# Attention scores of a float32 decoder trunk: 128-partition products with stacked keys in place of 64-partition tiles

## The chip, the cores and the metric

The kernel runs on one core of a Trainium2 chip. The metric is the device time of one execution in microseconds; of several runs the median is taken. A core has five engines that work side by side: TensorE (PE, matrix products; its weight loads are a row of their own, PEld), VectorE (DVE), ScalarE (ACT), GpSimd (POOL) and SyncE (SP, here it only issues DMAs).

## The reference

A trunk of two layers on one sequence of 1024 tokens with 1024 features, in float32. Layer 0 mixes by differential attention, layer 1 by causal pooling over windows of 2, 4, 8 and 16; both add an attention over 256 memory tokens, a gate and an output projection. What the change touches is the score of the differential attention: 12 heads, each with two maps of 64 features, rotated by position, and one value of 128 features.

```python
q = q.reshape(B, S, DA_HEADS, 2, DA_QK_DIM)      # 12 heads, 2 maps, 64
k = k.reshape(B, S, DA_HEADS, 2, DA_QK_DIM)
q = apply_rotary(q, cos, sin)
k = apply_rotary(k, cos, sin)
...
s = jnp.einsum('bqhmd,bkhmd->bhmqk', q_blk, k).astype(jnp.float32) * scale
s = jnp.where(mask, s, -jnp.inf)
p = jax.nn.softmax(s, axis=-1)
w = p[:, :, 0] - lam_full * p[:, :, 1]
return jnp.einsum('bhqk,bkhe->bqhe', w.astype(v.dtype), v)
```

## The kernel before, in words

Activations lie with features on partitions and tokens on the free axis, in two halves of 512 tokens. A float32 operand x of a product is split in two float32r parts, hi = round(x) and lo = x - hi, and a product takes three passes, hi*hi, hi*lo and lo*hi (`mm3`, lines 118 to 123).

The order of TensorE's work is written out by hand (`manual_schedule`, line 77); the instructions of the other engines are ordered by the scheduler. TensorE's base is a stream of projections, planned in `plan` (line 972): for each head the queries, the keys, a gate and the values of the next head, 16 steps of three 512-wide products each. `step(n)` issues the next n steps of it. Between the steps stands the work of the head in hand. `attention_layer` (line 1062) walks each head in 10 positions, one for each pair of query blocks and pair of key blocks: it transposes a block of weights (`turn_weights`, line 885), applies the block turned before (`apply_weights`, line 912), and at the positions listed in `ahead` (line 1065) issues the scores of one query block, some of them for the next head already.

A projected query or key leaves PSUM through `query_evac` (line 768) or `key_evac` (line 787). Both begin with `rotary` (line 755): four ACT copies of 32 partitions swap the halves of the features, DVE multiplies by the cosines, POOL multiplies the swapped copy by the sines, DVE adds. Then the operands of the scores are made, for each map on its 64 partitions:

- the stationary query tile `qa`: hi on the map's own 64 partitions, lo on the other 64 (two ACT and two DVE instructions a half; the factor -1/8 is taken in here);
- the moving key tile `kb`: hi on both halves of the partitions, and a second tile `kl` with the lo of both maps (four ACT copies and two DVE subtractions a half).

`scores` (line 831) takes for each half of the keys two PSUM banks out of three, one for each map. First come two products over 128 partitions ([hi; lo] of the query with [hi; hi] of the key, line 848), then two over 64 partitions (hi of the query with lo of the key, line 853): map 0 on partitions 0 to 63, map 1 on 64 to 127. The width is the number of keys in reach, 256 to 512. DVE adds the mask and takes the row minimum (line 857), two steps of the stream follow, and after both halves ACT takes the exponential with its sum (line 866). `combine` (line 872) makes the difference of the two maps on POOL (line 878) and DVE (line 881).

`prologue` (line 343) fills the start: hidden state, rotary tables (`rope_tables`, whose positions are loaded by a DMA that POOL issues, line 552) and the queries and keys of head 0. Line 297 fills the mask on POOL before that. `reuse_waits="tile"` (line 1067) lets the tiles of later stages take the space of attention tiles as each comes free.

Of the kernel before, what the change touches and what calls it, by code (L numbers as in the profile page):

```python
# [10 lines left out]
F32 = mybir.dt.float32  # L11
# [9 lines left out]
P = 128  # L21
# [27 lines left out]
class Trunk:  # L49
    """Activations are held as [feature on partitions, token on the free axis].  # L50

    A float32 operand x of a matrix product is held as two float32r parts,
    hi = round(x) and lo = x - hi; a product takes the passes hi*hi, hi*lo
    and lo*hi."""
# [49 lines left out]
    def load_split(self, wf, name, cols=D, dve=0, parts=1):  # L104
        """Weights of up to D columns as hi and lo, in parts; VectorE makes the first dve
        columns of lo of each part."""
        nc = self.nc
        wh = self.wpool.tile([P, D], F32R, tag="wh", name=f"wh_{name}")
        wl = self.wpool.tile([P, D], F32R, tag="wl", name=f"wl_{name}")
        n = cols // parts  # L110
        for lo in range(0, cols, n):
            nc.scalar.copy(wh[:, lo : lo + n], wf[:, lo : lo + n])  # L112
            for eng, c in ((nc.vector, slice(lo, lo + dve)), (nc.gpsimd, slice(lo + dve, lo + n))):
                if c.stop > c.start:
                    eng.tensor_tensor(wl[:, c], wf[:, c], wh[:, c].bitcast(F32), op=ALU.subtract)  # L115
        return wh, wl

    def mm3(self, out, sh, sl, mh, ml, first, last):
        """out (+)= s^T m over one contraction tile; s stationary, m moving."""
        nc = self.nc  # L120
        nc.tensor.matmul(out, sh, mh, start=first, stop=False)  # L121
        nc.tensor.matmul(out, sh, ml, start=False, stop=False)  # L122
        nc.tensor.matmul(out, sl, mh, start=False, stop=last)  # L123

# [1 line left out]
    def step(self, n):  # L126
        """Issues the next n steps (of three products with 512 columns) of the stream."""
        self.owed += n
        while self.owed >= 1:
            self.owed -= 1  # L130
            self.count += 1
            if next(self.stream, None) is None:
                self.owed = 0
                return
# [12 lines left out]
    def between(self, fn):  # L147
        """Adds work that is no projection to the stream."""

        def run(w):  # L150
            fn()
            return iter(())

        self.jobs.append((lambda: None, run))
# [17 lines left out]
    def projection(self, src, name, evac, halves=(1, 0)):  # L172
        """Adds the projection onto one tile of columns to the stream."""

        def run(w):
            for half in halves:
                yield from self.project(w, half, name, evac, self.sb if name == "v0" else None)

        self.jobs.append((lambda: self.load_w(src, name), run))

    def projection_pair(self, specs, first, second):
        """Two projections, half 1 of both before half 0, with the calls of first
        and second after the half 1 of each."""
# [33 lines left out]
    def rsqrt_small(self, pool, ms, n, tag, rest=None):  # L217
        """(ms + rest + EPS)^-0.5 of [P, n] tiles of PSUM."""
        x = pool.tile([P, n], F32, tag=f"rsx{tag}", name=f"rsx{tag}")
        self.nc.vector.tensor_scalar(x, ms if rest is None else rest, EPS, None, op0=ALU.add)  # L220
        if rest is not None:
            self.nc.vector.tensor_tensor(x, x, ms, op=ALU.add)
        return self.newton(pool, x, n, tag)

    def newton(self, pool, x, n, tag):
        """x^-0.5 of a [P, n] tile."""
# [13 lines left out]
    def mean_square(self, sqs, ones, n, name, bank=None):  # L240
        """[P token, n] means over the partitions of the sum of sqs, each [P, n*P]."""
# [10 lines left out]
    def diagonals(self, pool, r, n, tag, eng=None):  # L252
        """hi and lo of diag(r[:, j]) for j < n, r being [P, n]."""
# [16 lines left out]
    def spread(self, ds, n, name):  # L270
        """[P, n*P] in PSUM: the diagonals along the free axis, on all partitions."""
# [7 lines left out]
    def broadcast(self, pool, r, n, tag, eng=None):  # L279
        """[P, n*P] in PSUM with r [P token, n] along the free axis, on all partitions."""  # L280
        return self.spread(self.diagonals(pool, r, n, tag, eng), n, f"bc{tag}")

# [60 lines left out]
    def prologue(self, pool):  # L343
        """The first hidden state and the first two projections."""
# [65 lines left out]
    def memory_jobs(self, l):  # L410
        """Adds the keys and values of the memory for layer l to the stream: keys, values."""
# [77 lines left out]
    def mem_means(self):  # L489
        """1 / rms of the memory tokens: by token (rsm), and on all partitions (rsmb)."""  # L490
# [9 lines left out]
    def new_hidden(self, half, d, x, g):  # L500
        """Splits x * g of one [P, HALF] tile into the operands of the next projections."""
# [9 lines left out]
    def accumulate_square(self, pool, x, sums, d, name, tags, alone=False, by=None, add=None):  # L511
        """Adds the squares of tile d of a half to sums; those of the last tile can stay alone."""
# [13 lines left out]
    def row_means(self, pool, sums, half, rest=None):  # L526
        """1 / rms of the tokens of one half, by token; rest: what is to be added to the means."""
# [4 lines left out]
    def row_spread(self, half):  # L532
        """1 / rms of the tokens of one half, on all partitions, in PSUM."""
# [12 lines left out]
    def rope_tables(self, sp):  # L546
        """cos and sin of [32 frequencies on partitions, token], repeated 4 times; worked
        out with a quarter of the tokens on each 32 partitions."""
# [47 lines left out]
    def gate_evac(self, get, box, name):  # L596
        """2 * silu of one projected tile, by halves."""
# [56 lines left out]
    def mem_scores(self, pool, nm, q, kv):  # L654
        """softmax of the scores of 4 query blocks, as [P query, 4, MEM], times 0.5."""
# [47 lines left out]
    def mem_units(self, pool, layer, gates, starts):  # L703
        """The memory attention of all heads, between steps of the stream: the
        unit (head, half) number i goes on when the stream has come to starts[i]."""
# [41 lines left out]
    def play(self, events, until=None):  # L747
        """Issues the events that are due before the stream has come to the step until."""
# [6 lines left out]
    def rotary(self, pool, half, out, name):  # L755
# [4 lines left out]
        for b in range(4):  # L760
            o, i = b * 32, (b ^ 1) * 32
            nc.scalar.copy(rot[o : o + 32, :], out[i : i + 32, :])
        nc.vector.tensor_tensor(f, out, self.cosr[:, cols], op=ALU.mult)
# [4 lines left out]
    def query_evac(self, h, box):  # L768
        """Stationary operands of the scores: [hi; lo] of map 0, [lo; hi] of map 1."""
        nc = self.nc  # L770

        def evac(half, out):
            pool = self.apool
            f = self.rotary(pool, half, out, f"q{h}")
            t = pool.tile([P, 2, HALF], F32R, tag="ka", bufs=3, name=f"qa{h}{half}")
            lo, hi = slice(0, 64), slice(64, 128)
            for m, own, other in ((0, lo, hi), (1, hi, lo)):
                nc.scalar.activation(t[own, m, :], f[own, :], AF.Copy, scale=-QSCALE)
                nc.vector.scalar_tensor_tensor(
                    t[other, m, :], f[own, :], -QSCALE, t[own, m, :].bitcast(F32),  # L780
                    op0=ALU.mult, op1=ALU.subtract,
                )
            box[half] = t
# [3 lines left out]
    def key_evac(self, h, box):  # L787
        """Moving operands: [hi; hi] of each map, and lo of both maps."""
        nc = self.nc

        def evac(half, out):
# [3 lines left out]
            u = pool.tile([P, HALF], F32R, tag="kl", bufs=3, name=f"kl{h}{half}")  # L795
            lo, hi = slice(0, 64), slice(64, 128)
            for m, own, other in ((0, lo, hi), (1, hi, lo)):
                nc.scalar.copy(t[own, m, :], f[own, :])
                nc.scalar.copy(t[other, m, :], f[own, :])  # L799
                nc.vector.tensor_tensor(  # L800
                    u[own, :], f[own, :], t[own, m, :].bitcast(F32), op=ALU.subtract
                )
            box[half] = (t, u)
# [27 lines left out]
    def scores(self, pool, h, i, q, k, st):  # L831
        """exp(score - max) of query block i for both maps, and their row sums."""
# [9 lines left out]
        for kh in range(2 if n > HALF else 1):  # L842
            lo, hi = kh * HALF, min(n, (kh + 1) * HALF)
            kb, kl = k[kh]
            w = slice(0, max(hi - lo, 256))
            sc = [self.sb(f"s{h}{i}{m}{kh}") for m in range(2)]
            for m in range(2):
                nc.tensor.matmul(  # L848
                    sc[m][:, w], q[half][:, m, qs], kb[:, m, w], start=True, stop=False
                )  # L850
            for m in range(2):
                own = slice(64 * m, 64 * m + 64)
                nc.tensor.matmul(  # L853
                    sc[m][:, w], q[half][own, m, qs], kl[own, w], start=False, stop=True
                )
# [16 lines left out]
    def combine(self, i, es, st):  # L872
        """softmax(map 0) - lambda * softmax(map 1) of query block i, in place of map 0."""
# [11 lines left out]
    def turn_weights(self, pool, h, p, jj, w):  # L885
        """[P key, 2 key blocks, 256 query] of the weights of a pair of query blocks."""
# [43 lines left out]
    def attend_post(self, pool, h, half, o, g):  # L930
# [12 lines left out]
        def norm():  # L943
            """The squares summed over the partitions stand on all of them: a quarter of
            the tokens is worked on in each quarter of the partitions."""
# [19 lines left out]
    def run_hooks(self):  # L965
        """Issues what else waits for TensorE, at most one of a kind, when it is due."""
# [5 lines left out]
    def plan(self):  # L972
        """The order of all projections."""
# [88 lines left out]
    def attention_layer(self):  # L1062
        tc = self.tc
        # query blocks whose scores are issued in each of the 10 steps of a head
        ahead = {0: [(0, 2)], 1: [(0, 5)], 2: [(0, 3)], 4: [(0, 0)], 5: [(1, 6)], 6: [(0, 1)], 7: [(1, 7)], 9: [(1, 4)]}
        order = [(p, jj) for p in (3, 2, 1, 0) for jj in range(p + 1)]
        with tc.tile_pool(name="attn", bufs=1, reuse_waits="tile") as pool:
            self.apool = pool
            self.prologue(pool)
# [159 lines left out]
    def out_jobs(self, layer):  # L1229
# [17 lines left out]
        def operand(half, r, t):  # L1247
            """hi and lo of one tile of z; those of layer 1 stay on chip."""
# [175 lines left out]
```

## Time and profile before

| | us |
|---|---|
| three runs | 1879.61, 1881.83, 1885.98 |
| median | 1881.83 |
| span of the profiled execution, first to last instruction | 1881.1 |
| PE busy in it | 1815.2 |
| DVE busy | 1198.1 |
| ACT busy | 899.2 |
| POOL busy | 724.5 |

For the profiled execution the span is the only time that is recorded. It lies between the lowest and the median of the runs. Attention with its start takes the first 885 us or so, the memory's keys and values, the output projection of layer 0, the pooling layer and the last projection the rest.

How to read the rows: a row of a timeline has the start, the duration, engine, source line and operation, what is written and read, the shape, and the idle time of the engine before it with what ended it. Products are pipelined and their ends are modelled, so a 512-wide product shows 0.39 us though the next one starts sooner; the distance from start to start tells what one occupies. A weight load belongs to each product and normally runs during the product before.

### The profile page before, as it was taken

Reading aid. Unit: us, or ns where it says so; the run is one execution under the profiler, and the core shown is the slowest. Engines: PE = TensorE matmul, PEld = TensorE weight load, DVE = VectorE, ACT = ScalarE, POOL = GpSimd, SP = SyncE. Lnnn points to the kernel's source line nnn. Section 1 sums busy time; section 2 is a strip of 40 time slices with the busy share of each in tenths; the row PEclk is TensorE's granted clock in tenths of the full one; section 3 lists DMA queues with packets and bytes.
Section 4 is the critical chain, followed back from the end, with each engine's and each line's share of the span. In section 5 each row is a group of like instructions: output and inputs, shape, how many; then the busy total and the mean of one; then the engine's idle time right before and its main releaser. Section 6 shows DMA issues by size and latency. Waiting matters only on the chain. (4 is left out here: it accounts for less than half of the span.)

```text
span 1881.1 us, 24840 instructions
## 1 busy us (share of the span) xinstructions
PE 1815.2 (96%) x8670; PEld 1457.0 (77%) x8670; DVE 1198.1 (64%) x2446; ACT 899.2 (48%) x1649; POOL 724.5 (39%) x610
## 2 busy tenths in 40 slices
PE   7899999999999999999999999999999999999997
PEld 5577778777777777778788777778887777877885
DVE  7678778778778778876656768645453435454413
ACT  6566566666566657654246655524321112124422
POOL 3244334434444444433253343333332435512452
PEclk9899999999999999999999999999999999999998
DMA  5001111111101111112464769642212121245542
GB/s 181 23 34 39 52 45 51 42 44 57 46 34 57 46 44 47 46 46 68 157 207 140 240 223 301 221 138 93 90 37 94 46 72 58 68 149 201 179 145 95
DMA packets 80956, 186.04 MB, mean 99 GB/s; under 512 B 9120, under 2 KB 17024, under 8 KB 80832
## 3 DMA queue, kind: packets, MB, share of 16 engines
q1 hardware_dynamic: 79440, 182.04, 29.3%
q10 hardware_dynamic: 1296, 2.17, 0.3%
q8 instruction: 68, 1.11, 0.2%
q0 software_dynamic: 96, 0.26, 0.1%
q14 instruction: 56, 0.46, 0.1%
HBM read 152.67 MB, written 31.77 MB: 98 GB/s over the span
## 5 line engine op out<-in xcount | busy, mean ns | idle before, releaser
L866 ACT ACTIVATE e<-e,st 128x640 f32<-128x640 f32 (+4 forms) x192 | 148.2, 773 | 95.9 <-DVE st L857 95.0
L115 POOL TENSOR_TENSOR wl_o<-wf_o,wh_o 128x384 fp32r<-128x384 f32 x64 | 97.3, 1520 | 215.3 <-ACT wh_o L112 199.9
L878 POOL TENSOR_SCALAR e<-e,st 128x640 f32<-128x640 f32 (+4 forms) x96 | 80.7, 841 | 200.1 <-DVE st L877 87.2
L1264 DVE TENSOR_TENSOR zr<-zf,zr 128x512 fp32r<-128x512 f32 x132 | 113.8, 881 | 29.6 <-ACT zr L1263 29.2
L115 DVE TENSOR_TENSOR wl_o<-wf_o,wh_o 128x640 fp32r<-128x640 f32 x64 | 60.2, 940 | 109.3 <-ACT wh_o L112 102.6
L112 ACT CAST wh_o<-wf_o 128x1024 fp32r<-128x1024 f32 x64 | 67.3, 1052 | 113.4 <-PE ob L122 65.2
L857 DVE CUSTOM_DVE_ANT_0 e<-s,mask 128x512 f32<-128x512 f32 (+2 forms) x192 | 107.8, 585 | 16.7 <-PE s L853 15.4
L1263 ACT CAST zr<-zf 128x512 fp32r<-128x512 f32 x132 | 80.7, 620 | 71.8 <-DMA zf<-z 35.7
L906 ACT CAST wth<-wt 128x512 fp32r<-128x512 f32 (+2 forms) x168 | 72.1, 429 | 87.1 <-PE wt L903 71.9
L121 PE MATMUL ga<-hh,wh_ga 128*128 128x512 f32 x256 | 107.9, 422 | 4.2 <-DVE mqf L625 4.2
L121 PE MATMUL pga<-hh,wh_pga 128*128 128x512 f32 x256 | 100.5, 393 | 6.8 <-DVE pz L1188 4.9
L123 PE MATMUL ga<-hh,wl_ga 128*128 128x512 f32 x256 | 101.2, 395 | 0.0
L122 PE MATMUL ga<-hl,wh_ga 128*128 128x512 f32 x256 | 100.9, 394 | 0.0
L122 PE MATMUL ob<-zr,wh_o 128*128 128x512 f32 x256 | 100.3, 392 | 0.0
L121 PE MATMUL ob<-zr,wh_o 128*128 128x512 f32 x256 | 100.3, 392 | 0.0
L123 PE MATMUL ob<-zr,wl_o 128*128 128x512 f32 x256 | 100.3, 392 | 0.0
L122 PE MATMUL pga<-hl,wh_pga 128*128 128x512 f32 x256 | 99.8, 390 | 0.0
L123 PE MATMUL pga<-hh,wl_pga 128*128 128x512 f32 x256 | 99.7, 390 | 0.0
L907 DVE TENSOR_TENSOR wtl<-wt,wth 128x512 fp32r<-128x512 f32 (+2 forms) x168 | 83.1, 495 | 15.1 <-ACT wth L906 14.3
L121 PE MATMUL k<-hh,wh_k 128*128 128x512 f32 x192 | 83.9, 437 | 8.5 <-ACT wh_k L112 7.9
L881 DVE SCALAR_TENSOR_TENSOR e<-e,st,e 128x640 f32<-128x640 f32 (+4 forms) x96 | 82.1, 855 | 9.8 <-POOL e L878 9.0
L848 PE MATMUL s<-kb,qa 128*128 128x512 f32 (+2 forms) x288 | 81.4, 357 | 5.1 <-ACT kb L799 2.7
(283 smaller groups left out, 5480.1 us busy)
## 6 DMA issues: line engine op xcount, KB each, us to landing
zf<-z SPq DMA_DIRECT2D x132, 256.0 KB, 3.9
wf_o<-in_w_out SPq DMA_DIRECT2D x64, 512.0 KB, 3.6
wf_ga<-in_w_in SPq DMA_DIRECT2D x16, 512.0 KB
wf_pga<-in_w_in SPq DMA_DIRECT2D x16, 512.0 KB, 4.3
wf_q<-in_w_in SPq DMA_DIRECT2D x12, 512.0 KB, 3.2
wf_v<-in_w_in SPq DMA_DIRECT2D x12, 512.0 KB, 4.0
z<-rs SPq DMA_DIRECT2D x24, 256.0 KB, 3.2
z<-z SPq DMA_DIRECT2D x24, 256.0 KB, 2.0
```

The lines of the kernel that those rows point to most:

```text
L115: eng.tensor_tensor(wl[:, c], wf[:, c], wh[:, c].bitcast(F32), op=ALU.subtract)
L121: nc.tensor.matmul(out, sh, mh, start=first, stop=False)
L122: nc.tensor.matmul(out, sh, ml, start=False, stop=False)
L123: nc.tensor.matmul(out, sl, mh, start=False, stop=last)
L848: nc.tensor.matmul(sc[m][:, w], q[half][:, m, qs], kb[:, m, w], start=True, stop=False)
L857: nc.vector.tensor_tensor_reduce(out=es[m][:, lo:hi], in0=sc[m][:, : hi - lo], in1=self.mask[:, S - n + lo : S - n + hi], scale=1.0, scala ...
L866: nc.scalar.activation(es[m][:, :n], es[m][:, :n], AF.Exp, bias=least[m], scale=-1.0, accum_out=st[:, 2, m : m + 1],)
L878: nc.gpsimd.tensor_scalar(es[1][:, :n], es[1][:, :n], st[:, 3, 1:2], 1.0, op0=ALU.mult, op1=ALU.mult)
L881: nc.vector.scalar_tensor_tensor(es[0][:, :n], es[0][:, :n], st[:, 3, 0:1], es[1][:, :n], op0=ALU.mult, op1=ALU.add)
L907: nc.vector.tensor_tensor(wl[:, lo:hi], t[:, lo:hi], wh[:, lo:hi].bitcast(F32), op=ALU.subtract)
L1263: nc.scalar.copy(z[:, 0, :], zf)
L1264: nc.vector.tensor_tensor(z[:, 1, :], zf, z[:, 0, :].bitcast(F32), op=ALU.subtract)
```

## The change

The scores keep four products a group, and all run over 128 partitions. The key tile holds [hi; lo] of each map, so that `kl` goes. The query tile `qa` holds [hi; hi], and a second tile holds [lo; zeros], so that the two passes give hi*hi + hi*lo and lo*hi. The tiles with the zeros are four fixed ones, filled on POOL before the prologue; each half of a head writes only the 64 partitions of lo. The two passes of a map now follow each other, map 0 before map 1. The factor -1/8 moves into `rotary`, whose product with the cosines becomes an instruction with a scalar and two tensors for keys and queries alike. The scratch space of POOL's own DMAs is set to 4096, which frees space for the new tiles. The docstrings and comments are dropped without effect on the program.

```diff
-    def rotary(self, pool, half, out, name):
+    def rotary(self, pool, half, out, name, scale=1.0):
...
-            nc.scalar.copy(rot[o : o + 32, :], out[i : i + 32, :])
-        nc.vector.tensor_tensor(f, out, self.cosr[:, cols], op=ALU.mult)
+            nc.scalar.activation(rot[o : o + 32, :], out[i : i + 32, :], AF.Copy, scale=scale)
+        nc.vector.scalar_tensor_tensor(
+            f, out, scale, self.cosr[:, cols], op0=ALU.mult, op1=ALU.mult
+        )
...
     def query_evac(self, h, box):
...
-            f = self.rotary(pool, half, out, f"q{h}")
+            f = self.rotary(pool, half, out, f"q{h}", -QSCALE)
             t = pool.tile([P, 2, HALF], F32R, tag="ka", bufs=3, name=f"qa{h}{half}")
+            z = self.qlo[(2 * h + 1 - half) % len(self.qlo)]
             lo, hi = slice(0, 64), slice(64, 128)
             for m, own, other in ((0, lo, hi), (1, hi, lo)):
-                nc.scalar.activation(t[own, m, :], f[own, :], AF.Copy, scale=-QSCALE)
-                nc.vector.scalar_tensor_tensor(
-                    t[other, m, :], f[own, :], -QSCALE, t[own, m, :].bitcast(F32),
-                    op0=ALU.mult, op1=ALU.subtract,
-                )
-            box[half] = t
+                nc.scalar.copy(t[own, m, :], f[own, :])
+                nc.scalar.copy(t[other, m, :], f[own, :])
+                nc.vector.tensor_tensor(
+                    z[own, m, :], f[own, :], t[own, m, :].bitcast(F32), op=ALU.subtract
+                )
+            box[half] = (t, z)
...
     def key_evac(self, h, box):
...
-            u = pool.tile([P, HALF], F32R, tag="kl", bufs=3, name=f"kl{h}{half}")
             lo, hi = slice(0, 64), slice(64, 128)
             for m, own, other in ((0, lo, hi), (1, hi, lo)):
                 nc.scalar.copy(t[own, m, :], f[own, :])
-                nc.scalar.copy(t[other, m, :], f[own, :])
                 nc.vector.tensor_tensor(
-                    u[own, :], f[own, :], t[own, m, :].bitcast(F32), op=ALU.subtract
+                    t[other, m, :], f[own, :], t[own, m, :].bitcast(F32), op=ALU.subtract
                 )
-            box[half] = (t, u)
+            box[half] = t
...
     def scores(self, pool, h, i, q, k, st):
...
-            for m in range(2):
-                nc.tensor.matmul(
-                    sc[m][:, w], q[half][:, m, qs], kb[:, m, w], start=True, stop=False
-                )
-            for m in range(2):
-                own = slice(64 * m, 64 * m + 64)
-                nc.tensor.matmul(
-                    sc[m][:, w], q[half][own, m, qs], kl[own, w], start=False, stop=True
-                )
+            for m in range(2):
+                for part in range(2):
+                    nc.tensor.matmul(
+                        sc[m][:, w], q[half][part][:, m, qs], k[kh][:, m, w],
+                        start=(part == 0), stop=(part == 1),
+                    )
...
     def attention_layer(self):
...
+            self.qlo = [pool.tile([P, 2, HALF], F32R, name=f"qlo{i}") for i in range(4)]
+            for z in self.qlo:
+                nc.gpsimd.memset(z[64:128, 0, :].bitcast(F32), 0.0)
+                nc.gpsimd.memset(z[0:64, 1, :].bitcast(F32), 0.0)
             self.prologue(pool)
...
-    nc = bacc.Bacc("TRN2", target_bir_lowering=False, num_devices=1)
+    nc = bacc.Bacc(
+        "TRN2", target_bir_lowering=False, num_devices=1, dynamic_dma_scratch_size=4096
+    )
```

More of the change, by code (lines that the diff above doesn't have):

```diff
@@ L843, in scores @@
             lo, hi = kh * HALF, min(n, (kh + 1) * HALF)
-            kb, kl = k[kh]
             w = slice(0, max(hi - lo, 256))
@@ L1062, in attention_layer @@
     def attention_layer(self):
-        tc = self.tc
+        tc, nc = self.tc, self.nc
         ahead = {0: [(0, 2)], 1: [(0, 5)], 2: [(0, 3)], 4: [(0, 0)], 5: [(1, 6)], 6: [(0, 1)], 7: [(1, 7)], 9: [(1, 4)]}
```

## The prediction

> **What bounds the kernel now.** I read the page first (busy shares), then the busy times by stretch, then the groups by form for the two lines of score products, then the TensorE timeline around single score blocks, and last the timelines of the other engines around the operands of the scores.
>
> ```profile
> span 1881.1 us, 24840 instructions
> PE 1815.2 (96%) x8670; PEld 1457.0 (77%) x8670; DVE 1198.1 (64%) x2446; ACT 899.2 (48%) x1649; POOL 724.5 (39%) x610
> ...
> 135.00:885.00 750.00, 747.63 (x3796) 588.11 (x3795) 589.21 (x1518) 465.72 (x915) 309.69 (x305) 1.00 0.14 48
> 885.00:1100.00 215.00, 206.76 (x1065) 173.02 (x1064) 137.47 (x228) 98.89 (x191) 79.51 (x72) 0.99 0.54 178
> ```
>
> The first two lines are the page's; the others give length, then PE, weight load, DVE, ACT, POOL busy, granted clock, DMA share and GB/s. In the steady attention stretch PE is covered for 747.63 of 750 us at full clock; DVE, the next, for 589.21 (79%). So the length of PE's own list sets the end of this stage, and one microsecond taken out of that list should leave the span, as long as what feeds PE keeps up. But "busy" has modelled ends. What a product occupies is better read from start to start.
>
> The changed products are all in this stage. By form (line 848 is the first pass of the scores over 128 partitions, line 853 the second pass over 64):
>
> ```profile
> L853 PE MATMUL s<-kl,qa 64*128 64x512 f32 x144 | 36.2, 500 | 0.0
> L853 PE MATMUL s<-kl,qa 64*128 64x256 f32 x96 | 18.5, 382 | 0.0
> L853 PE MATMUL s<-kl,qa 64*128 64x384 f32 x48 | 10.6, 440 | 0.0
> ```
>
> Two of these belong to one group of four score products, so there are 72 groups 512 wide, 48 of 256 and 24 of 384. Now one group of each width in PE's timeline (start, duration; "x2" is two instructions merged), then a pair of 256-wide products of line 926, and last the weight loads of the first group:
>
> ```profile
> 511.90 0.39 PE L123 MATMUL k<-hh,wl_k 128*128 128x512 f32 x1
> 512.13 0.63 PE L848 MATMUL s<-kb,qa 128*128 128x512 f32 x2
> 512.69 0.51 PE L853 MATMUL s<-kl,qa 64*128 64x512 f32 x2
> 513.12 0.50 PE L121 MATMUL k<-hh,wh_k 128*128 128x512 f32 x1
> 513.46 0.39 PE L122 MATMUL k<-hl,wh_k 128*128 128x512 f32 x1
> ...
> 500.12 0.40 PE L848 MATMUL s<-kb,qa 128*128 128x256 f32 x2
> 500.45 0.39 PE L853 MATMUL s<-kl,qa 64*128 64x256 f32 x2
> 500.77 0.50 PE L121 MATMUL q<-hh,wh_q 128*128 128x512 f32 x1
> 501.10 0.40 PE L122 MATMUL q<-hl,wh_q 128*128 128x512 f32 x1
> ...
> 506.62 0.52 PE L848 MATMUL s<-kb,qa 128*128 128x384 f32 x2
> 507.07 0.44 PE L853 MATMUL s<-kl,qa 64*128 64x384 f32 x2
> 507.44 0.50 PE L121 MATMUL q<-hh,wh_q 128*128 128x512 f32 x1
> 507.79 0.39 PE L122 MATMUL q<-hl,wh_q 128*128 128x512 f32 x1
> ...
> 504.08 0.40 PE L926 MATMUL o<-wth,vh 128*128 128x256 f32 x2
> 504.32 0.40 PE L926 MATMUL o<-wth,vl 128*128 128x256 f32 x2
> ```
>
> ```profile
> 512.69 0.19 PEld L853 LDWEIGHTS s<-kl,qa 64*128 64x128 f32 x2 [0.37 <-issue]
> 513.12 0.19 PEld L121 LDWEIGHTS k<-hh,wh_k 128*128 128x128 f32 x1 [0.25 <-issue]
> ```
>
> A full 512-wide product takes a slot of 0.23 us (511.90 to 512.13), a full 256-wide one 0.12 (two in 504.08 to 504.32). Around line 853 this rhythm breaks at both edges: the second pass starts 0.56 after the first instead of 0.46, its weight load begins only with it, after 0.37 us in which the weight path did nothing, and the product after it again has its load unprepared (0.25 idle) and needs 0.34 instead of 0.23. In between, the two 64-partition products of the pair run at once: both weight loads lie within 0.19 us and the pair leaves PE after 0.43. So line 853 has a gain (two products in one slot) and a cost (two edges).
>
> **The change, part by part.** *TensorE.* Four products stay four, all over 128 partitions and each with its own weights. I price a group as regular slots, from its first product to the second product after it: at 512, 513.46 - 512.13 = 1.33 us against 5 x 0.23 = 1.15, gain 0.18, times 72 is 13.0. At 256, 501.10 - 500.12 = 0.98 against 4 x 0.12 + 0.23 = 0.71, gain 0.27, times 48 is 13.0. At 384, 507.79 - 506.62 = 1.17 against 4 x 0.175 + 0.23 = 0.93 (0.175 is an estimate halfway between the two slots), gain 0.24, times 24 is 5.8. Sum **31.8 us**. That regular slots return is taken from the row of line 848 itself, which follows a projection 0.23 us after it, and from line 926, whose 256-wide products change weights every time and hold 0.12.
> The trace shows that a switch between tile shapes idles the weight path. The Trainium skill, "TensorEngine Tiling (Array Packing)", Key Properties, says that changing the tiling mode drains TensorE while tiles of one mode load and multiply in parallel; by it both edges go, the trace agrees with 0.37 and 0.25 us of idle weight path, and the sum stays at 31.8.
>
> *Operands of the keys.* Before, four ACT copies and two DVE subtractions a half; after, two copies and two subtractions, and the first product needs both halves of the tile, so PE now waits for DVE where it waited for ACT; behind it stands all of PE's list, since that order is written by hand. The tightest place, the second half of the next head's keys before its block 6:
>
> ```profile
> 536.23 0.62 ACT L798 CAST kb<-fk 64x512 fp32r<-64x512 f32 x1 [0.98 <-DVE fk L765]
> 536.88 0.62 ACT L799 CAST kb<-fk 64x512 fp32r<-64x512 f32 x1
> 536.88 0.68 DVE L800 TENSOR_TENSOR kl<-fk,kb 64x512 fp32r<-64x512 f32 x1
> ...
> 538.16 0.62 ACT L799 CAST kb<-fk 64x512 fp32r<-64x512 f32 x1
> 538.17 0.69 DVE L800 TENSOR_TENSOR kl<-fk,kb 64x512 fp32r<-64x512 f32 x1 [0.53 <-ACT kb L798]
> 538.60 0.74 PE L848 MATMUL s<-kb,qa 128*128 128x512 f32 x2
> ...
> 522.42 1.32 DVE L881 SCALAR_TENSOR_TENSOR e<-e,st,e 128x768 f32<-128x768 f32 x1
> ...
> 525.57 0.60 PE L903 MATMUL wt<-cst,e 128*128 128x128 f32 x4
> ```
>
> Now the last copy ends at 538.78, just as PE begins. After: copies 536.23 to 536.85 and 536.88 to 537.50, subtractions 536.88 to 537.56 and 537.56 to about 538.25, if DVE takes them at once. The second map's product comes third in the new order, two slots after the first, so it has about 0.8 us to spare, less some 0.3 that PE arrives earlier (one 256-wide group lies between). I take no new wait. The last two rows give another margin: the weights of block 5 are ready at 523.74 and turned at 525.57, 1.83 us; the groups between shorten that by about half a microsecond.
>
> Lower bound for these waits:
>
> ```profile
>   DVE st L857: 8.5, 20
>   ACT kb L799: 8.5, 12
> ```
>
> These are the waits in front of line 848, loads and products counted together. The first map's bank is complete two products earlier, so DVE can free it earlier, and the key copies shrink; both can go in part. I take 0, with -8 as the lower end.
>
> *Operands of the queries.* ACT gets eight instructions a half instead of six (two copies more, like those of 0.62 us), the keys two fewer, so ACT's sum is unchanged. DVE keeps four, with the scale now in the product with the cosines:
>
> ```profile
> L763 DVE TENSOR_TENSOR fq<-q,trig_tab 128x512 f32<-128x512 f32 x24 | 16.6, 691 | 14.1 <-ACT rotq L762 13.7
> L939 DVE SCALAR_TENSOR_TENSOR og<-o,subln,gaa 128x512 f32<-128x512 f32 x24 | 17.9, 746 | 7.5 <-ACT sq L938 7.4
> ```
>
> The form it takes, read from PSUM, costs 746 ns against 691: 48 x 0.055 = 2.6 us more on DVE, hidden under PE; if that cover were gone it costs just these 2.6.
>
> *Zeros and space.* Eight fills of 64x512 on POOL at the very start:
>
> ```profile
> 0.74 0.95 POOL L297 MEMSET mask<- 128x1024 bf16 x1 [0.29 <-POOLq L1411]
> 1.64 0.73 POOL L552 DMA_DIRECT2D pos_i<-in_positions  x1
> ...
> 7.43 1.27 POOL L524 TENSOR_TENSOR ssqx<-ssqx,ssqx 128x512 f32<-128x512 f32 x1 [4.12 <-ACT ssqx L520]
> ...
> 7.91 0.80 PE L121 MATMUL k<-hh,wh_k 128*128 128x512 f32 x1 [7.91 <-ACT wh_k L112]
> ```
>
> Fills of about 0.5 (half the columns of line 297) to 0.95 us make 4 to 7.6. POOL is idle for 4.12 us before 7.43. Behind them queue the issue of the positions (line 552), on which the rotary tables and through DVE's queue the first hidden state wait, and the first squares. Fully exposed: 7.6; fully covered: 0. I take 1.5, nearer to the idle stretch. The smaller scratch space for POOL's own DMAs touches two issues of this kind, both at the start, and I give it nothing (0.73 if one is issued again). The new tiles take 10 KB a partition more than those they replace and move later tiles; the stretch after attention has 8 us of idle PE (215 - 206.76), and a third of it either way is in the range.
>
> Sum against this execution's span: 1881.1 - 31.8 + 1.5 = 1850.8; the median of the three runs is 0.7 above that span, so 1851.
>
> **The rivals.**
> *A, slower: the parallel pair is lost and the edges stay.* If the idle at the edges belongs to how the score operands are read or signalled and not to the tile's shape, every group gains a slot: 72 x 0.23 + 48 x 0.12 + 24 x 0.175 = 26.5 us, 1908. For it: the pair visibly runs at once. Against it: line 848 reads the same query tile and starts in rhythm, and the product after line 853, which belongs to a projection, is late too. At 512 the edges cost 1.33 - 4 x 0.23 = 0.41 and the parallel slot is worth 0.23, so it decides once more than half of the edge cost stays. The Trainium skill, "TensorE: Matmul & The Clock Gate", Part 3, holds that row tiles run concurrently and a small contraction alone costs as much as a full one; by this rule alone the change goes the way of A. Chance 0.06.
> *B, waits behind DVE take the gain.* The subtraction of the keys, or the row minimum, falls behind a 1.32 us item such as that of line 881, at 12 heads and two places of each: 24 x (1.32 - 0.8) = 12.5 us; behind two such items at one place 12 x (2.64 - 0.8) = 22. Time 1863 to 1873. For it: DVE's list is in fixed order, and at 79% of a shorter stage it would be at 82%. Against it: the margins above. Chance 0.12.
> *C, no change: half of the edge cost stays.* Edge costs worked out as in A are 0.41 at 512, 0.98 - (3 x 0.12 + 0.23) = 0.39 at 256 and 1.17 - (3 x 0.175 + 0.23) = 0.415 at 384. With half of each gone and the parallel slot lost, the gain is 72 x (0.205 - 0.23) + 48 x (0.195 - 0.12) + 24 x (0.21 - 0.175) = 2.6 us; less 1.5 at the start, about 1881 on the median. For and against it stands what stands at A. Chance 0.03. That 64-partition tiles remain can be excluded: the new slices take all partitions.
>
> **How the numbers follow.** My forecast has 0.79. Its own range is 1842 (waits gone) to 1858 (start exposed). The range takes in the first part of B: 1842 to 1866. This kernel's measurement can tell about 0.3%, 5.6 us, from no change; forecast and B are faster by more, so 0.91, C 0.03 within, A 0.06 slower.
>
> **What would show it.** Right: no product with 64 partitions; a 512-wide group and the next product in 1.15 us from start to start, a 256-wide one in 0.71; the next product's load prepared during the group; the attention stage some 32 us shorter with DVE near 82%; all later stages as long as now. Wrong: groups of 1.5 us or more (A); regular groups but PE idle in front of line 848's successor or of the turns, ended by DVE (B); a first product on PE well after 7.91, or longer later stages, which would put the start or the moved tiles in doubt.

## The result and the profile after

The changed kernel takes 1852.24 us in the median (1851.81 to 1856.59, four runs) against 1883.15 for the kernel before (1879.61 to 1885.98, four runs). The ratio is 0.9842, with a 95% interval from 0.9824 to 0.9860: 1.6% faster. In a later comparison on another chip the same kernel (e13) took 1859.40 us, and its ratio was 0.9854 (0.9833 to 0.9876); so between the experiments below, which ran on several chips, the ratios compare better than the microseconds. The profiled execution has a span of 1850.1 us.

The page and the busy times of the attention stretch, now 135 to 860 us (line 851 issues all score products now):

```profile
span 1850.1 us, 24825 instructions
PE 1778.2 (96%) x8670; PEld 1479.3 (80%) x8670; DVE 1223.2 (66%) x2446; ACT 899.7 (49%) x1649; POOL 724.1 (39%) x618
...
135.00:860.00 725.00, 716.18 (x3781) 606.81 (x3781) 609.94 (x1508) 463.69 (x912) 305.28 (x304) 1.00 0.14 50
```

PE has as many instructions as before and is busy 37 us less. DVE stands at 84% of this stretch (79% before), and over the whole span it is busy 25 us more, with as many instructions; where these come from stands in the last section. PE is covered for 716.18 of 725 us, where 747.63 of 750 were covered before: there is idle time now that was not there.

TensorE's timeline around one group of 512 and one of 256, and the weight load of the projection after the first:

```profile
492.93 0.39 PE L851 MATMUL s<-kb,qa 128*128 128x512 f32 x1
493.16 0.39 PE L851 MATMUL s<-kb,qlo 128*128 128x512 f32 x1
493.39 0.39 PE L851 MATMUL s<-kb,qa 128*128 128x512 f32 x1
493.62 0.39 PE L851 MATMUL s<-kb,qlo 128*128 128x512 f32 x1
493.85 0.39 PE L121 MATMUL k<-hh,wh_k 128*128 128x512 f32 x1
494.08 0.39 PE L122 MATMUL k<-hl,wh_k 128*128 128x512 f32 x1
...
495.24 0.28 PE L851 MATMUL s<-kb,qa 128*128 128x256 f32 x1
495.36 0.28 PE L851 MATMUL s<-kb,qlo 128*128 128x256 f32 x1
495.48 0.28 PE L851 MATMUL s<-kb,qa 128*128 128x256 f32 x1
495.60 0.29 PE L851 MATMUL s<-kb,qlo 128*128 128x256 f32 x1
495.72 0.40 PE L121 MATMUL k<-hh,wh_k 128*128 128x512 f32 x1
495.97 0.39 PE L122 MATMUL k<-hl,wh_k 128*128 128x512 f32 x1
```

```profile
493.62 0.19 PEld L121 LDWEIGHTS k<-hh,wh_k 128*128 128x128 f32 x1
```

From the first score product to the second product after the group it is 494.08 - 492.93 = 1.15 us at 512 (1.33 before) and 495.97 - 495.24 = 0.73 at 256 (0.98 before). At 384 it is 488.57 - 487.64 = 0.93 (1.17 before). The load of the projection's weights runs at 493.62, during the last score product, and no longer stands open behind it.

What TensorE lost in the score groups did not all come off the span. The time splits at the first and the last score product; these rows of the two lines of before, and the first and last of line 851 of after, have the starts in the middle ("first to last start"):

```profile
L848 PE MATMUL s<-kb,qa x288: 277/395/770, 65.2 to 879.6; 128*128 128x512 f32 x72, 128*128 128x256 f32 x48, 128*128 128x384 f32 x24
L853 PE MATMUL s<-kl,qa x288: 379/476/792, 67.2 to 879.8; 64*128 64x512 f32 x72, 64*128 64x256 f32 x48, 64*128 64x384 f32 x24
```

```profile
L851 PE MATMUL s<-kb,qa x288: 278/392/522, 60.9 to 849.5; 128*128 128x512 f32 x72, 128*128 128x256 f32 x48, 128*128 128x384 f32 x24
L851 PE MATMUL s<-kb,qlo x288: 277/393/522, 61.3 to 849.7; 128*128 128x512 f32 x72, 128*128 128x256 f32 x48, 128*128 128x384 f32 x24
...
  DVE kb L803: 2.6, 3
```

| | before | after | difference |
|---|---|---|---|
| start to the first score product | 65.2 | 60.9 | -4.3 |
| first to last score product | 814.6 | 788.8 | -25.8 |
| last score product to the end | 1001.3 | 1000.4 | -0.9 |

The last row of the fence is what is left of the waits in front of the score products: 2.6 us, where there were twice 8.5 (loads and products together). From start to start of TensorE's products, what exceeds the regular distance inside the groups adds up to 0.8 us, against 5.3 before. In place of these waits there is a new one, at one place in ten of the twelve heads. Waits of PE in 135 to 850 us, and that place in one head, the turn of the weights of blocks 4 and 5:

```profile
PE wt L902 <- DVE e L880: 8.4, 10, 1.0
```

```profile
503.50 0.91 POOL L877 TENSOR_SCALAR e<-e,st 128x768 f32<-128x768 f32 x1 [3.32 <-DVE st L876]
503.86 0.69 DVE L235 TENSOR_TENSOR rsua<-rsx,rsya 128x128 f32<-128x128 f32 x1
504.37 1.34 POOL L767 TENSOR_TENSOR rotk<-rotk,trig_tab 128x512 f32<-128x512 f32 x1
504.47 0.68 DVE L764 SCALAR_TENSOR_TENSOR fk<-k,trig_tab 128x512 f32<-128x512 f32 x1
505.07 0.79 DVE L236 SCALAR_TENSOR_TENSOR rsua<-rsua,rsya 128x128 f32<-128x128 f32 x1
...
505.78 1.01 DVE L880 SCALAR_TENSOR_TENSOR e<-e,st,e 128x768 f32<-128x768 f32 x1
505.80 0.27 PE L902 MATMUL wt<-cst,e 128*128 128x128 f32 x1
...
506.85 0.55 PE L902 MATMUL wt<-cst,e 128*128 128x128 f32 x3 [0.78 <-DVE e L880]
```

PE turns block 4 at 505.80 and stands until 506.85 for block 5, whose weights DVE finishes at 506.79. POOL was done with its part at 504.41; DVE took the rotation of the keys and two pieces of the norm (lines 235 and 236) first. These two pieces took 0.69 and 0.79 us, while POOL scaled the weights and multiplied the keys by the sines; the same two lines took 0.29 each at 501.63 and 501.95, with POOL idle. Their 0.90 us more are nearly as much as the lack. Counted as before, from the end of DVE's part to the first transpose, the margin of 1.83 us became a lack of 1.0. From start to start, the distances between the transposes of the turns add up to 47.4 us, 11.6 more than before (35.8).

### The profile page after: what moved, and what is told of

Its sections match the earlier page's. It is cut to its first block, busy times and chain, and to the rows that moved or that the text cites. A ratio compares the mean times of both kernels' runs of the same rounds, so it can differ in the third digit from the quotient of the medians.

```text
span 1850.1 us, 24825 instructions
## 1 busy us (share of the span) xinstructions
PE 1778.2 (96%) x8670; PEld 1479.3 (80%) x8670; DVE 1223.2 (66%) x2446; ACT 899.7 (49%) x1649; POOL 724.1 (39%) x618
## 5 line engine op out<-in xcount | busy, mean ns | idle before, releaser
L877 POOL TENSOR_SCALAR e<-e,st 128x640 f32<-128x640 f32 (+4 forms) x96 | 76.3, 795 | 198.0 <-DVE st L876 115.5
L121 PE MATMUL ga<-hh,wh_ga 128*128 128x512 f32 x256 | 104.0, 406 | 3.5 <-DVE mqf L625 3.5
L851 PE MATMUL s<-kb,qa 128*128 128x512 f32 (+2 forms) x288 | 98.5, 349 | 0.9 <-DVE kb L803 0.9
L851 PE MATMUL s<-kb,qlo 128*128 128x512 f32 (+2 forms) x288 | 98.4, 349 | 0.0
L121 PE MATMUL k<-hh,wh_k 128*128 128x512 f32 x192 | 79.2, 412 | 8.5 <-ACT wh_k L112 8.5
```

The source lines that it names most:

```text
L851: nc.tensor.matmul(sc[m][:, w], q[half][part][:, m, qs], k[kh][:, m, w], start=(part == 0), stop=(part == 1),)
L877: nc.gpsimd.tensor_scalar(es[1][:, :n], es[1][:, :n], st[:, 3, 1:2], 1.0, op0=ALU.mult, op1=ALU.mult)
```

## Experiments

**The shape alone, there and back.** The changed kernel with its second pass on the 64 partitions that are not zero, both maps side by side (e1) and map by map (e2).

```diff
-            for m in range(2):
-                for part in range(2):
+            for part in range(2):                  # e2: the two loops as in the changed kernel
+                for m in range(2):
+                    own = slice(64 * m, 64 * m + 64) if part else slice(0, P)
                     nc.tensor.matmul(
-                        sc[m][:, w], q[half][part][:, m, qs], k[kh][:, m, w],
+                        sc[m][:, w], q[half][part][own, m, qs], k[kh][own, m, w],
```

> The changed kernel with its second pass cut back to the 64 partitions that are not zero, both maps side by side as in the kernel before. Theory (the edges belong to the tile shape): groups return to 1.33, 1.17 and 0.98 us with the product after them, 31.8 us more PE time than 1852; where PE is later, the new wait of the turns (11.9 us) may shrink, so 1872 to 1884. Rival (the edges came from how the old operands were read or signalled): the pair in one slot and no edges, 26.5 us less than 1852, about 1826.

> The same 64-partition second pass, but map by map (128, 64, 128, 64 partitions): no pair, four changes of shape in a group instead of two. Theory: each group is regular slots plus twice the edge cost (0.82 us at 512, 0.78 at 256, 0.83 at 384), 72 x 0.82 + 48 x 0.78 + 24 x 0.83 = 116 us more than 1852, less the waits that a later PE no longer meets: 1955 to 1968. Rival (edges not from the shape): about 1852.

e1: 1873.44 us, ratio to the kernel before 0.9945 (0.9920 to 0.9971). e2: 1955.64, ratio 1.0364 (1.0340 to 1.0389). e1 lies where the theory put it. e2 lies at the lower edge of its range; by its ratio, which gives some 1952 us, a few microseconds below it. A 512-wide group of each in TensorE's timeline:

```profile
511.93 0.63 PE L852 MATMUL s<-kb,qa 128*128 128x512 f32 x2
512.49 0.50 PE L852 MATMUL s<-kb,qlo 64*128 64x512 f32 x2
512.92 0.50 PE L121 MATMUL k<-hh,wh_k 128*128 128x512 f32 x1
513.25 0.40 PE L122 MATMUL k<-hl,wh_k 128*128 128x512 f32 x1
```

```profile
518.68 0.40 PE L852 MATMUL s<-kb,qa 128*128 128x512 f32 x1
519.00 0.50 PE L852 MATMUL s<-kb,qlo 64*128 64x512 f32 x1
519.43 0.50 PE L852 MATMUL s<-kb,qa 128*128 128x512 f32 x1
519.86 0.50 PE L852 MATMUL s<-kb,qlo 64*128 64x512 f32 x1
520.29 0.50 PE L121 MATMUL v<-hh,wh_v 128*128 128x512 f32 x1
520.63 0.39 PE L122 MATMUL v<-hl,wh_v 128*128 128x512 f32 x1
```

With the same operands as in the changed kernel, the group of e1 takes 513.25 - 511.93 = 1.32 us, that of the kernel before. In e2, with four changes of shape and no pair, it takes 1.95 (1.97 expected), and each product between two changes takes 0.43 instead of 0.23. e1 differs from the changed kernel in the order of the products too; e2 differs in the shape of the second pass alone. So the edges belong to the change of shape, not to operands or signals, and rival A is out: that row tiles run at once, on which it rested, holds (the two products of e1's pair start within 0.01 us of each other), but does not pay here. The drain on a change of mode that the Trainium skill names ("TensorEngine Tiling (Array Packing)", Key Properties) agrees with this; its size here is 0.4 us for a change there and back, more than the one slot of 0.23 that the pair saves.

e1 has no wait at the turn. There the margin is still positive:

```profile
514.66 2.06 DVE L881 SCALAR_TENSOR_TENSOR e<-e,st,e 128x768 f32<-128x768 f32 x1
...
517.20 0.60 PE L903 MATMUL wt<-cst,e 128*128 128x128 f32 x4
```

517.20 - 516.72 = 0.48 us. Of the 1.35 us between 1.83 and 0.48, DVE's sum itself takes 0.74: 2.06 us here against 1.32 before, both times beside POOL's product with the sines, and 1.01 in the changed kernel, where POOL is idle. The rest comes with the new operands and the order that the scheduler makes of them. From 0.48 to -1.0 it comes with the change of shape, but not by PE's pace alone: in the changed kernel DVE rotates the keys ahead of this sum (504.47), in e1 behind it (516.64). How much each of these takes is not separated.

**Putting the block ahead.** The combination of block 5 at high priority (e3), or its scores one position earlier and those of block 2 one later (e4).

```diff
-                self.combine(i, es, st)
+                with tc.high_priority(offset=SOON):      # e3, for i == 5
+                    self.combine(i, es, st)
...
-        ahead = {0: [(0, 2)], 1: [(0, 5)],
+        ahead = {0: [(0, 5)], 1: [(0, 2)],              # e4
```

> The changed kernel with the combination of block 5 (reciprocal, factor, POOL scaling, DVE sum) put ahead by priority. Theory (the 1.05 us wait of each head's turn of blocks 4 and 5 comes from their place in DVE's order behind the rotation and the norms): that wait goes, 11 x 1.05 = 11.6 us less, about 1841. Rival (the engines have no room there; what is moved back makes PE wait elsewhere): 1848 to 1856.

> The changed kernel with the scores of block 5 issued one position earlier in each head, those of block 2 one later. Theory: the margin before the turn of blocks 4 and 5 grows by about 6.7 us, the wait goes, about 1841. Rival (the five large weight buffers are the limit, block 5 then waits for one to come free): no gain or slower, 1850 to 1865.

e3: 1857.62, ratio 0.9849 (0.9831 to 0.9867), the wait as it was (9.7 us in this trace, 8.4 and 9.7 in the two of the changed kernel); the theory is out. e4: 1868.09, ratio 0.9897 (0.9872 to 0.9923): the wait at the turn is gone, as the theory has it, and a larger one stands before the second map's products, for a PSUM bank that DVE has not yet read, not for a weight buffer as the rival had it:

```profile
PE s L851 <- DVE st L856: 14.4, 20, 1.1
```

So the place of block 5 sets where PE waits; that nothing else was short is refuted.

**Taking work from the engines.** The second query copy on POOL (e6), the lo of the queries on POOL (e11), the norm's small instructions later (e9).

```diff
-                nc.scalar.copy(t[other, m, :], f[own, :])            # in query_evac
+                nc.gpsimd.tensor_copy(t[other, m, :], f[own, :])     # e6
...
-                nc.vector.tensor_tensor(
+                nc.gpsimd.tensor_tensor(                             # e11
                     z[own, m, :], f[own, :], t[own, m, :].bitcast(F32), op=ALU.subtract
...
-DUE = 7
+DUE = 14                                                             # e9
```

> The changed kernel with the second query copy of each map (hi onto the other 64 partitions) made by POOL instead of ACT. Theory (two more ACT copies, 1.24 us, stand in front of block 5's exponentials and take that much of the margin before the turn of blocks 4 and 5): the exponentials start 1.2 us earlier, the 1.05 us wait of each head goes, about 1841. Rival (DVE's order, not ACT's, sets that wait): the wait stays near 1 us, 1850 to 1856.

> The changed kernel with the lo of the queries subtracted on POOL instead of DVE, 48 instructions and some 43 us less on DVE. Theory (the wait of the turn is DVE's lack of room): the wait goes, about 1841. Rival (POOL, which scales the weights of block 5, is then late in its place): the wait stays or grows, 1852 to 1868.

> The changed kernel with the norm of an output half due 14 steps after it instead of 7, which takes its chain of small DVE instructions away from block 5. Theory (DVE's order sets the wait of the turn): the wait goes, about 1841. Rival (ACT's copies set it, DVE follows): the wait stays, 1850 to 1856; the norms landing on another tight place would show as a new wait.

All three missed 1841. e6: 1865.8, ratio 0.9889 (0.9861 to 0.9918). e11: 1888.62, ratio 1.0014 (0.9994 to 1.0034). e9: 1900.55, ratio 1.0082 (1.0055 to 1.0109). All three lie outside of their rivals' ranges too. In e6 the wait at the turn is 8.4 us in total, as in the changed kernel, and 6.3 us of waits for banks come on top. PE's waits of e11 and of e9:

```profile
PE wt L902 <- DVE e L880: 20.1, 10, 2.0
```

```profile
PE s L851 <- DVE st L856: 25.3, 26, 1.9
```

Without the ACT copies the wait at the turn is the same, so these copies alone do not set it. With the norm's chain moved away it is gone, so what stands on DVE's list ahead of the block matters; but the chain then lands where PE waits for banks. In e11 the wait doubles, though DVE has fewer instructions. One head of it:

```profile
524.01 0.91 POOL L877 TENSOR_SCALAR e<-e,st 128x768 f32<-128x768 f32 x1
...
525.00 1.29 POOL L785 TENSOR_TENSOR qlo<-fq,qa 64x512 fp32r<-64x512 f32 x1
525.09 1.35 DVE L235 TENSOR_TENSOR rsua<-rsx,rsya 128x128 f32<-128x128 f32 x1
...
528.97 1.01 DVE L880 SCALAR_TENSOR_TENSOR e<-e,st,e 128x768 f32<-128x768 f32 x1
```

POOL has scaled the weights by 524.92, so it is not late, as the rival had it. DVE adds them only from 528.97 on: a piece of the norm takes 1.35 us instead of 0.29 beside the subtraction that was moved to POOL, and two more, at 524.15 and 527.41, take 0.91 and 1.02 beside other work of POOL. Work given to POOL thus came back as longer instructions on DVE.

**The shape with the old operands.** Queries [hi; lo], keys [hi; hi] and [lo; zeros]: the roles exchanged in `query_evac` and `key_evac`, and

```diff
-                        sc[m][:, w], q[half][part][:, m, qs], k[kh][:, m, w],
+                        sc[m][:, w], q[half][:, m, qs], k[kh][part][:, m, w],
```

> The changed kernel with the roles exchanged: queries [hi; lo] (two ACT copies), keys [hi; hi] and [lo; zeros] (four ACT copies), so that ACT and DVE have their work as in the kernel before and only the shape of the second pass differs. Theory (of the margin of 1.83 us before the turn of blocks 4 and 5, the moved ACT copies took 1.35, as the paired run shows with 0.48, and the faster PE the other 1.53): with 0.3 us of margin left no wait, 11.6 us less than 1852, up to 4.4 us of the old waits back: 1841 to 1846. Rival (the faster PE alone brings the wait): 1850 to 1856.

e10: 1874.52, ratio 0.9932 (0.9909 to 0.9955), outside of both. The wait at the turn is gone (the weights are ready 0.6 us before), and others took its place, for banks and for the projection of the gate behind the keys' rotation:

```profile
PE s L851 <- DVE st L856: 10.0, 10, 1.2
PE ga L121 <- DVE fk L764: 6.2, 10, 0.6
```

These waits lie earlier in the head and give DVE time, so this run does not settle how much of the lost margin is due to the operands and how much to PE's pace.

**PE's own order.** The turn of blocks 4 and 5 two steps later (e12), and the changed kernel again beside it (e13).

```diff
-                turn(k + 1)
+                if g != 3:
+                    turn(k + 1)
...
                 self.step(1)
+                if g == 3:
+                    turn(k + 1)
                 self.apply_weights(p, jj, turned.pop(k), self.qkv[h][2], o)
```

> The changed kernel with the turn of blocks 4 and 5 issued two steps of the stream later in TensorE's own order (1.38 us), nothing moved on the other engines by hand. Theory (the weights of block 5 come 1.05 us after PE's place for their turn, nothing else is short): the wait goes, 11.6 us less, ratio to the kernel before about 0.978, 1841. Rival (the order that the scheduler then finds puts another wait in its place, as in the runs before): 1850 to 1865.

> The changed kernel itself, beside the late turn on the same chip: ratio to the kernel before 0.984, as at first.

e12: 1874.81, ratio 0.9938 (0.9915 to 0.9961). e13: 1859.40, ratio 0.9854 (0.9833 to 0.9876). e12 is slower than its rival's range too. Again the wait goes and another comes, longer:

```profile
PE ga L121 <- DVE fk L764: 12.7, 10, 2.1
```

None of these orders is faster than that of the changed kernel, and e3 cannot be told from it.

**The start.** The kernel before with only the fills and the smaller scratch space (e7), and the changed kernel with its fills behind the positions (e8).

```diff
+            for i in range(4):                                       # e7, in the kernel before
+                z = pool.tile([P, HALF], F32R, name=f"qlo{i}")
+                nc.gpsimd.memset(z[64:128, :].bitcast(F32), 0.0)
+                nc.gpsimd.memset(z[0:64, :].bitcast(F32), 0.0)
             self.prologue(pool)
+            for z in self.qlo:                                       # e8: moved behind it
+                ...
```

> The kernel before with nothing added but eight fills of 64x512 at the head of POOL's list and the smaller scratch space; the filled tiles are not used. As the prediction priced it: 0 to 7.6 us slower, 1.5 taken, about 1884. Rival (behind the fills the positions land later, the rotary tables' instructions leave DVE free for the first hidden state, and the start gets shorter by the 4.3 us seen in the changed kernel): about 1878 to 1880.

> The changed kernel with the eight fills behind the issue of the positions on POOL instead of ahead of it. If the fills ahead of the positions shortened the start: the first score again at about 65 us and 4 us more, about 1856. Rival (the start's length comes from elsewhere, such as when the clock is granted): 1850 to 1853.

e7: 1883.01, ratio 0.9985 (0.9965 to 1.0005), which does not separate it from no change; the upper end is 0.9 us, below the 1.5 that the prediction took. In its trace the first score product starts at 62.5 us. One of its twelve executions took 4531.51 us and is not in the ratio; nothing here explains it. e8: 1862.69, ratio 0.9876 (0.9853 to 0.9900), first score product at 65.2. POOL's timeline of the changed kernel, then DVE's of the changed kernel and of e8:

```profile
6.12 0.73 POOL L552 DMA_DIRECT2D pos_i<-in_positions  x1
```

```profile
18.75 0.28 DVE L558 CAST angle<-pos_i 128x256 f32<-128x256 int32 x1
```

```profile
6.90 0.62 DVE L558 CAST angle<-pos_i 128x256 f32<-128x256 int32 x1 [0.47 <-DMA pos_i<-in_positions]
```

The fills hold back the issue of the positions by 4.5 us (1.64 in the kernel before), and the scheduler then puts the rotary tables' instructions on DVE behind part of the hidden state (18.75 instead of 6.90). With the fills first, the first score product starts at 60.4 to 63.7 us in twelve traces (60.9 and 62.4 in the two of the changed kernel); without them, in the kernel before and in e8, at 65.2. So the start is 1.5 to 4.8 us shorter with the fills first. That it is so because PE then gets the hidden state earlier is argued: PE's waits for it on DVE are 2.2 us before and 1.9 after. Whole times do not settle the difference, since e8's interval overlaps both of the changed kernel's.

## Why the prediction was right, point by point

**The groups.** 31.8 us were forecast from the slots and edges. The groups measure 1.15, 0.73 and 0.93 where 1.15, 0.71 and 0.93 stood, which by these rows makes 13.0 + 12.0 + 5.8 = 30.8 us. e1, with the old shape and the new operands, has the old group again, and e2, which differs in the shape alone, shows the price of each change. Between e1 and the changed kernel the ratios differ by 0.0103, some 19 us (the profiled spans, on two chips, by 1871.1 - 1850.1 = 21.0): the gain of the groups less most of the wait that the faster products meet.

**New waits.** Taken as 0 and mis-sized: 11.6 us of wait at the turn, less some 4.5 us of old waits in front of the score products, net some 7 us lost. It is the mechanism of rival B, at less than its price of 12.5 us, at the place for which the prediction had quoted a margin of 1.83 us and allowed half a microsecond; the runs show 2.8 lost. The step that failed is the reading of that margin as fixed: it hung on DVE's order and on what POOL does at the same time, and both changed. Of the signs that the prediction named, the regular groups came, but so did a sign of B, PE idle before the turns until DVE is done; the stage got 25.8 us shorter, not 32.

**The keys.** No wait for the subtractions on DVE was forecast, and 2.6 us in 3 places are left, against a lower end of -8 for both kinds together. At the place that the prediction called the tightest, the last subtraction ends at 519.02 and the first product starts at 519.54, so the reading of it came out. The time of a subtraction was mis-sized: 0.68 us was taken, and the mean of the 48 is 1.14. That did not reach PE here.

**The start.** Priced at 1.5 us, between 0 and 7.6; it came out shorter by 4.3 (2.8 in the second trace of the changed kernel). That the positions queue behind the fills was seen, but only as a cost; a bound below zero was missing. Why the start gets shorter is argued, not shown.

**The rest.** ACT's busy time stays (899.2 before, 899.7 after), and what follows the last score product differs by 0.9 us. The product with the cosines takes 690 ns in its new form where 746 were allowed, so the 2.6 us more on DVE did not come; DVE has 25 us more for another reason, its longer instructions beside POOL. The sum, 1850.8 against a span of 1850.1, is closer than its terms, and that is luck: from the first to the last score product 25.8 us came off instead of 31.8, and a start 5.8 us better than priced makes up for it. Gain and waits of that stretch, 30.8 less 7, leave some 2 us that these rows do not assign.

## What to carry to other kernels

Two 64-partition products side by side save one slot (0.23 us at 512 columns), but a list of 128-partition products pays for leaving and re-entering the full shape (0.41); price both from start to start before splitting a product, and count how many small products share one change. Once the bound engine is 4% faster, the margins of the second engine decide what arrives, and in a schedule that a planner remakes they move with any edit: measure them again rather than carry them over. And before moving work from DVE to POOL, look at what DVE does at that time: its instructions can get longer by as much as was taken off it.

## What the runs showed of the hardware that was not expected

The cost of a change of shape depends little on the width: 0.41, 0.415 and 0.39 us for 512, 384 and 256 columns, there and back. The 384 rests on the prediction's estimated slot of 0.175 us, and the changed kernel has it: four such products take 0.70 us (487.64 to 488.34). So a change costs about 0.2 us whatever the width. In e2, where each change stands alone, the same price holds: 1.95 us for a 512-wide group against 1.15 without, 0.20 for each of four changes.

Some DVE instructions take longer beside work of POOL. The key subtractions, before and after, and the longest of them in one head of the changed kernel:

```profile
L800 DVE TENSOR_TENSOR kl<-fk,kb 64x512 fp32r<-64x512 f32 x48 | 32.9, 686 | 6.2 <-ACT kb L798 5.3
L803 DVE TENSOR_TENSOR kb<-fk,kb 64x512 fp32r<-64x512 f32 x48 | 54.5, 1136 | 1.5
...
510.39 2.81 POOL L115 TENSOR_TENSOR wl_v<-wf_v,wh_v 128x1024 fp32r<-128x1024 f32 x1 [1.07 <-ACT wh_v L112]
510.99 2.77 DVE L803 TENSOR_TENSOR kb<-fk,kb 64x512 fp32r<-64x512 f32 x1
```

In ten heads one subtraction takes about 2.77 us, each time beside POOL's subtraction for the value weights; of the 48, none that ran with POOL idle took more than 0.69. The 21.6 us more of this line are most of the 25 that DVE is busy longer. In e4 and e6, where the order is another, the mean is 0.70 us again. The traces show that the two coincide; no run here moves POOL's work alone, so how far this sets the wait at the turn stays open.
